# Gate tables written in quarters, one-hot pairs built in two VectorE operations, and late loads issued from ScalarE, in a two-block transformer kernel

## The chip, the cores and the metric

The kernel runs on one core of a Trainium2 chip. The metric is the device time of one execution in microseconds (us), the median of several runs. A profiled execution also leaves a trace of every instruction and every transfer. PE is TensorE's matrix multiply, PEld its weight load, DVE is VectorE, ACT is ScalarE, POOL is GpSimd, SP is SyncE; a trailing q (ACTq, SPq) means an engine's own instruction stream, where it issues transfers.

## The reference

Two blocks run one after the other on 512 tokens of width 1024 in float32. The first mixes tokens and then applies a product-key mixture of 16384 experts, each of which is one row of a table `peer_u` and one row of a table `peer_v`; the second has four mixer layers (pooling, short convolution, latent attention, pooling). The change touches the expert stage alone:

```
q = xb @ w_query                       # 8 heads, two halves of 128 columns
s = q . subkeys                        # 128 scores for each half
sv, si = top_k(s, 16)                  # best 16 of each half
top_s, pos = top_k(all 256 sums, 16)   # best 16 experts of each head
gates = softmax(top_s)                 # 8 heads x 16 = 128 gates for a token
hid = gelu(u_table[experts] . xb) * gates
y   = hid @ v_table[experts]
```

## The kernel before

**Two ways to the same sum.** For the first 384 tokens (ND) the kernel does not gather experts. It multiplies all 16384 rows of the U table with the tokens, applies gelu, multiplies by a dense gate table (zero where an expert isn't chosen) and multiplies with all of the V table. That is 128 U tiles of 128 experts and 128 V tiles. The last 128 tokens are served by gathering: 128 U rows and 128 V rows of 512 KB for all of them, fetched by GpSimd and folded in by one VectorE operation each (line 737 for U, 743 and 745 for V; class `Few`, called with `few.upto`).

**Every weight tile** is loaded by SP (line 139, three buffers `wraw`), rounded by ScalarE into `whi` (141) and completed by VectorE as `wlo` (143); a product is three matmuls (147 to 149), so that a U or V tile is 24 matmuls of 384 columns. `next_w` keeps two tiles ahead of the one in work (`AHEAD`).

**`peer_early`.** After 16 query tiles, `experts_x` scales each of eight chunks of the tokens, splits it into `xh` and `xl` for the 384 tokens, and turns the other 128 tokens with PE (806) into `few.xg`. Then a loop over 96 U tiles (EARLY) does in each pass, in this order: matmuls of one U tile, gelu into `hid` (1002), a store of two tiles to `hid_d` in memory (1004), what the list `pend` holds, at most one gathered row, and then a portion of side work on VectorE, at least SIDE units of it. The side work is a list of generators: top-k of the four token groups, and `all_gates`, which builds the dense gates of a group of 128 tokens in blocks of eight tokens. A block is four VectorE operations (two for `oj` and `oe`, a comparison of positions with indices, 968 and 969; two for `oi`, multiplied by the gates' high and low parts, 972). In the next pass PE multiplies the block's one-hots (16 short matmuls, 979 and 980), ScalarE writes two results into `stg` (982), and after four blocks, ScalarE issues two stores of 1 MB from `stg` to `g_d` (988). `turn` (935) transposes the top-k's result on PE, and ScalarE copies it out; it stands in `pend`, so it runs in the pass after the one that ends a top-k.

**`peer_late`.** It works through eight groups of 16 tiles, first groups 6 and 7, whose U tiles were not done early (32 U tiles, with gelu at 1072 and gates at 1040), and then groups 0 to 5, whose results are read back. The V tiles of a group are two halves of eight tiles. In the second half before a group that was done early (`fetch`), each V tile also loads `hh` (1084, two U results) and every second tile loads `g` (1050, gates of four U tiles). Both are issued on SP, in program order with the weight tiles. Six halves are such fetching halves. Numbers in FEW_RATE spread the remaining gathered rows over the tiles: per tile 1.3 shares beside a U tile, 1.6 beside a plain V tile and 0.3 beside a fetching one.

No scheduler reorders this part: each engine runs in the order in which the code issues (`manual_schedule`).

Of the kernel before, what the change touches and what calls it, by code (L numbers as in the profile page):

```python
# [42 lines left out]
SIDE = 2.6  # L43
AHEAD = 2
EARLY = 96
FEW_EARLY = 64
# [33 lines left out]
def tile_model(ctx: ExitStack, tc: tile.TileContext, xT, cst, vec, pos, w_in, w_tok, w_out, w_q, subk,  # L80
# [674 lines left out]
    def peer_early(bp, hid_d, g_d, ahead, next_w, few):  # L755
        sk = bp.tile([128, 128, GB], F32, name="stg", bufs=2).rearrange("p (h c) n -> p h (c n)", h=32)[:, :16]
# [40 lines left out]
        def experts_x():  # L797

            pt = None
# [42 lines left out]
        iT = bp.tile([128, ND], F16, name="iT")  # L842
        jT = bp.tile([128, ND], F16, name="jT")
        gT = bp.tile([128, ND], F16, name="gT")
        gL = bp.tile([128, ND], F16, name="gL")

        def topk(tt):
# [82 lines left out]
            ts_ = slice(tt * 128, tt * 128 + 128)  # L930

            def turn():
# [3 lines left out]
                scalar.copy(iT[:, ts_], pt[:, 0:128])  # L936
                scalar.copy(jT[:, ts_], pt[:, 128:256])
                scalar.activation(gT[:, ts_], pt[:, 256:384], AF.Copy, scale=GSCALE)
                scalar.activation(gf[tt], pt[:, 256:384], AF.Copy, scale=GSCALE)

            gf[tt] = bp.tile([128, 128], F32, name="gf", bufs=2)
            pend.append(turn)
# [3 lines left out]
        def all_gates(tt):  # L946
            ts_ = slice(tt * 128, tt * 128 + 128)
            vector.tensor_sub(gL[:, ts_], gf.pop(tt), gT[:, ts_])
            yield 0.3
            for nb in range(tt * 128 // GB, (tt + 1) * 128 // GB):  # L950
                yield from gates(nb)

        def gates(nb):


            stg = bp.tile([128, 128, GB], F32, name="stg", bufs=2)
            for h8 in range(GB // HB):
                ns = slice(nb * GB + h8 * HB, nb * GB + (h8 + 1) * HB)
                sh = [128, HB // 2, 128, 2]

                def pairs(t):
                    return t[:, ns].rearrange("p (a o b) -> p a o b", o=1, b=2).to_broadcast(sh)

                places = iotax[:, None, :, :].to_broadcast(sh)
                oj = bp.tile(sh, F16, name="oj", bufs=2)
                oe = bp.tile(sh, F16, name="oe", bufs=1)
                oi = [bp.tile(sh, F16, name="oi%d" % q, bufs=2) for q in range(2)]
# [6 lines left out]
                def dense(oj=oj, oi=oi, h8=h8, q4=0):  # L974
                    ps = ptile()
                    for q in range(4):
                        pq = ps[:, q * 128:(q + 1) * 128]
                        n = q4 * 4 + q
                        tensor.matmul(pq, oj[:, n // 2, :, n % 2], oi[0][:, n // 2, :, n % 2], start=True, stop=False)
                        tensor.matmul(pq, oj[:, n // 2, :, n % 2], oi[1][:, n // 2, :, n % 2], start=False, stop=True)  # L980
# [11 lines left out]
                yield 1.4  # L992

        pend = []
        hid = [None]
# [18 lines left out]
        while side or pend:  # L1014
            now, pend[:] = pend[:], []
            for f in now:
                f()
            some(2.4)
        return xn

    def peer_late(bp, hid_d, g_d, order, next_w, xn, few):
# [23 lines left out]
        queue = []  # L1045

        def get_gates(gr):

            t = bp.tile([128, ND // GB, 4, GB], F32, name="g", bufs=2)
            sync.dma_start(t, g_d[gr])  # L1050
            queue.append(t)

        gates_of = [4 * gr + i for gr in order for i in range(4)]

        def gates(q):

            if q % 4 == 0:
                if q or not queue:
                    queue and queue.pop(0)
                while len(queue) < 2 and gates_of:  # L1060
                    get_gates(gates_of.pop(0))
            return queue[0]

        parts = []
        for n, gr in enumerate(order):
            if gr * 16 >= EARLY:
                parts = []
                for q in range(16):
# [4 lines left out]
                    parts += weighted([a[:, :ND]], gates(q), q % 4)  # L1073
                    slot(0)
                queue.pop(0)
# [599 lines left out]
```

## Time and profile before

| | before |
|---|---|
| median of 3 runs | 3272.76 us (3271.66 to 3275.04) |
| the profiled execution's own time | 3275.82 us |
| its span, first to last instruction | 3274.1 us |
| PE busy | 3148.1 us, 96% of the span |
| DVE / ACT / POOL busy | 2199.2 / 1189.6 / 529.8 us |
| moved by DMA | 525.03 MB, 160 GB/s over the span |

The span is 1.7 us shorter than the execution's own time, which holds what lies around it. A busy PE does not mean that PE runs at its peak: the granted clock has two levels, 1.2 and 2.4 GHz, shown as 0.5 and 1.00 of full speed, and a stretch's clock is the mean of both. The expert stage lies between about 330 and 1721 us of the span; the early loop runs from 480 to 993 us and the late part from there to 1721 us.

### The profile page before, as it was taken

Reading aid. Unit: us, or ns where it says so; the run is one execution under the profiler, and the core shown is the slowest. Engines: PE = TensorE matmul, PEld = TensorE weight load, DVE = VectorE, ACT = ScalarE, POOL = GpSimd, SP = SyncE. Lnnn points to the kernel's source line nnn. Section 1 sums busy time; section 2 is a strip of 40 time slices with the busy share of each in tenths; the row PEclk is TensorE's granted clock in tenths of the full one; section 3 lists DMA queues with packets and bytes.
Section 4 is the critical chain, followed back from the end, with each engine's and each line's share of the span. In section 5 each row is a group of like instructions: output and inputs, shape, how many; then the busy total and the mean of one; then the engine's idle time right before and its main releaser. Section 6 shows DMA issues by size and latency. Waiting matters only on the chain.

```text
span 3274.1 us, 42422 instructions
## 1 busy us (share of the span) xinstructions
PE 3148.1 (96%) x16233; PEld 2720.5 (83%) x16233; DVE 2199.2 (67%) x3983; ACT 1189.6 (36%) x1785; POOL 529.8 (16%) x490
## 2 busy tenths in 40 slices
PE   8999989899998999999999999999999999999998
PEld 7787869888988999998997888888888777778887
DVE  5466779989776888887787665445446655666564
ACT  3334323354553333333334223222224434443222
POOL 2121100121113543332232001000002100010001
PEclk9999989999999999999999999999999999999999
DMA  3211215788888978888882222323332212222331
GB/s 114 71 59 36 88 64 181 238 283 264 268 275 299 372 280 334 324 330 314 320 281 85 96 95 95 94 95 93 96 97 69 71 58 72 72 82 90 97 97 64
DMA packets 194011, 525.03 MB, mean 160 GB/s; under 512 B 16656, under 2 KB 71184, under 8 KB 193680
## 3 DMA queue, kind: packets, MB, share of 16 engines
q1 hardware_dynamic: 99072, 341.86, 31.2%
q0 software_dynamic: 38144, 136.33, 12.0%
q10 hardware_dynamic: 56592, 44.13, 4.1%
q8 instruction: 127, 2.08, 0.3%
q14 instruction: 76, 0.62, 0.1%
HBM read 474.03 MB, written 46.14 MB: 159 GB/s over the span
## 4 chain that ended last, share of the span: by engine, by line
PE 61%; issue 20%; DVE 7%; POOL 6%; DMA 4%; ACT 2%; ACTq 0%; POOLq 0%; DVEq 0%
PE mm L147 18%; PE mm L149 18%; PE mm L148 17%; POOL row L724 5%; DMA row<-in_v_rows_dram,gi 4%; DVE wlo L143 2%; PE mm L1473 1%; PE mm L1440 1%; DVE row L737 1%; PE mm L438 1%; PE mm L1442 1%; PE mm L1459 1%; PE mm L177 0%; POOL acc L193 0%; DVE xg L745 0%
## 5 line engine op out<-in xcount | busy, mean ns | idle before, releaser
L147 PE MATMUL mm<-xh,whi 128*128 128x512 f32 (+2 forms) x2640 | 995.9, 377 | 14.4 <-ACT whi L141 10.3
L141 ACT CAST whi<-wraw 128x1024 fp32r<-128x1024 f32 (+1 forms) x586 | 588.4, 1006 | 1112.0 <-PE mm L148 489.8
L149 PE MATMUL mm<-xh,wlo 128*128 128x512 f32 (+2 forms) x2640 | 976.7, 370 | 15.9 <-DVE wlo L143 15.7
L148 PE MATMUL mm<-xl,whi 128*128 128x512 f32 (+2 forms) x2640 | 971.6, 368 | 1.7 <-DVE xl L227 1.6
L143 DVE TENSOR_TENSOR wlo<-wraw,whi 128x1024 fp32r<-128x1024 f32 (+1 forms) x586 | 687.3, 1174 | 345.6 <-ACT whi L141 344.0
L149 PEld LDWEIGHTS mm<-xh,wlo 128*128 128x128 f32 x2640 | 501.5, 190 | 90.0 <-DVE wlo L143 24.7
L147 PEld LDWEIGHTS mm<-xh,whi 128*128 128x128 f32 x2640 | 502.7, 190 | 83.5 <-ACT whi L141 12.2
L148 PEld LDWEIGHTS mm<-xl,whi 128*128 128x128 f32 x2640 | 502.8, 190 | 66.3 <-DVE xl L227 3.8
L149 PE MATMUL mm<-mh,wlo 128*128 128x384 f32 x1024 | 348.5, 340 | 11.3 <-DVE wlo L143 11.2
L147 PE MATMUL mm<-mh,whi 128*128 128x384 f32 x1024 | 347.0, 339 | 12.5 <-ACT whi L141 12.5
L148 PE MATMUL mm<-ml,whi 128*128 128x384 f32 x1024 | 345.8, 338 | 0.0
L724 POOL DMA_INDIRECT row<-in_u_rows_dram,gi x128 | 160.1, 1251 | 621.9 <-DVE row L737 386.8
L724 POOL DMA_INDIRECT row<-in_v_rows_dram,gi x128 | 173.1, 1352 | 347.7 <-DVE xg L745 317.4
L149 PEld LDWEIGHTS mm<-mh,wlo 128*128 128x128 f32 x1024 | 194.7, 190 | 19.8 <-DVE wlo L143 19.3
L147 PEld LDWEIGHTS mm<-mh,whi 128*128 128x128 f32 x1024 | 194.7, 190 | 16.0 <-ACT whi L141 16.0
L147 PE MATMUL mm<-mxh,whi 128*128 128x512 f32 x512 | 204.4, 401 | 0.0
L148 PE MATMUL mm<-mxl,whi 128*128 128x512 f32 x512 | 202.0, 395 | 0.0
L149 PE MATMUL mm<-mxh,wlo 128*128 128x512 f32 x512 | 201.9, 394 | 0.0
L237 DVE TENSOR_TENSOR H<-H,mm 128x512 f32<-128x512 f32 x144 | 98.8, 686 | 149.4 <-PE mm L149 149.0
L148 PEld LDWEIGHTS mm<-ml,whi 128*128 128x128 f32 x1024 | 194.8, 190 | 0.0
L745 DVE SCALAR_TENSOR_TENSOR xg<-row,actg,xg 128x1024 f32<-128x1024 f32 x127 | 163.5, 1288 | 24.4 <-DMA row<-in_v_rows_dram,gi 22.9
L737 DVE SCALAR_TENSOR_TENSOR row<-row,xg 128x1024 f32<-128x1024 f32 x128 | 154.7, 1218 | 5.6 <-DMA row<-in_u_rows_dram,gi 5.6
(357 smaller groups left out, 3848.4 us busy)
## 6 DMA issues: line engine op xcount, KB each, us to landing
wraw<-in_u_t_dram SPq DMA_DIRECT2D x128, 512.0 KB, 4.6
wraw<-in_v_t_dram SPq DMA_DIRECT2D x128, 512.0 KB, 6.2
wraw<-in_pw_in_dram SPq DMA_DIRECT2D x64, 512.0 KB, 3.5
wraw<-in_cw_in_dram SPq DMA_DIRECT2D x64, 512.0 KB, 3.5
g_d<-stg ACTq DMA_DIRECT2D x24, 1024.0 KB, 8.8
g<-g_d SPq DMA_DIRECT2D x32, 768.0 KB, 5.9
hid_d<-hid ACTq DMA_DIRECT2D x48, 384.0 KB, 5.1
hh<-hid_d SPq DMA_DIRECT2D x48, 384.0 KB, 5.4
```

The lines of the kernel that those rows point to most:

```text
L141: scalar.copy(hi[:, :n], raw[:, :n])
L143: vector.tensor_sub(lo[:, :n], raw[:, :n], hi[:, :n].bitcast(F32))
L147: tensor.matmul(ps, sh, mh, start=start, stop=False)
L148: tensor.matmul(ps, sh, ml, start=False, stop=False)
L149: tensor.matmul(ps, sl, mh, start=False, stop=stop)
L237: vector.tensor_tensor(h[2 * dp + e], h[2 * dp + e], ps, op=OP.add)
L438: tensor.matmul(pl[:, j * 64:(j + 1) * 64].rearrange("p (n b) -> p n b", b=b), kf[:, tiles[j]], pairs_of(q[:, j * 128:(j + 1) * 128], b)[: ...
L724: gpsimd.indirect_dma_start(out=t, out_offset=None, in_=table, in_offset=bass.IndirectOffsetOnAxis(ap=self.gi[:, j:j + 1], axis=0))
L737: vector.scalar_tensor_tensor(t, t, 1.0, self.xg, op0=OP.mult, op1=OP.mult, accum_out=hid[:, j:j + 1])
L745: vector.scalar_tensor_tensor(y, t, act[:, j:j + 1], y, op0=OP.mult, op1=OP.add)
L1440: tensor.matmul(ps[:, :nk], qn[e][:, qs], kn[e][:, :nk], start=True, stop=False)
L1442: tensor.matmul(ps[:, :nk], qr[e][rows, qs], krl[rows, :nk], start=False, stop=True)
```

## The change

1. A block's one-hots are two operations of 2048 elements instead of four of 1024: `oh` holds both comparisons and `og` both products; indices and gates lie in `keys` and `gts`, with the pairs side by side. A half block counts 1.25 units of side work instead of 1.4; SIDE goes from 2.6 to 2.75.
2. The store of a `stg` tile is four pieces of 512 KB, kept in a list `outs`. Each pass issues one piece right after its U tile; when a new `stg` tile is begun, all that are left are issued.
3. `turn` goes to a list `later` and runs one pass later.
4. FEW_EARLY goes from 64 to 48: 48 gathered rows in the early loop, 208 in the late part.
5. The late loads of `g` and `hh`: two of each are issued by SP at the start of the late part, every further one by ScalarE, right after it has used up the buffer's contents.
6. The eight token transposes leave `experts_x`: ScalarE copies the chunks aside, and `turn_x` transposes them after the second U tile.

```diff
-SIDE = 2.6
+SIDE = 2.75
-FEW_EARLY = 64
+FEW_EARLY = 48
...
                 xn.append(split(t[:, :ND], ND))
-                if kt % 4 == 0:
-                    pt = ptile()
-                tensor.transpose(pt[:, kt % 4 * 128:(kt % 4 + 1) * 128], t[:, ND:512], ident)
-                if kt % 4 == 3:
-                    scalar.copy(few.xg[:, (kt - 3) * 128:(kt + 1) * 128], pt)
+                scalar.copy(xt[:, kt], t[:, ND:512])
+
+        def turn_x():
+
+            for q in range(2):
+                pt = ptile()
+                for kt in range(4):
+                    tensor.transpose(pt[:, kt * 128:(kt + 1) * 128], xt[:, q * 4 + kt], ident)
+                scalar.copy(few.xg[:, q * 512:(q + 1) * 512], pt)
...
-            pend.append(turn)
+            later.append(turn)
...
+            while outs:
+                scalar.dma_start(*outs.pop(0))
             stg = bp.tile([128, 128, GB], F32, name="stg", bufs=2)
             for h8 in range(GB // HB):
...
-                vector.tensor_tensor(oj, places, pairs(jT), op=OP.is_equal)
-                vector.tensor_tensor(oe, places, pairs(iT), op=OP.is_equal)
-                yield 1.4
-                for q, g in enumerate((gT, gL)):
-                    vector.tensor_tensor(oi[q], oe, pairs(g), op=OP.mult)
+                oh = bp.tile(sh, F16, name="oh", bufs=2)
+                og = bp.tile(sh, F16, name="og", bufs=2)
+                vector.tensor_tensor(oh, iotax[:, None, None, :, :].to_broadcast(sh), pairs(keys), op=OP.is_equal)
+                yield 1.25
+                vector.tensor_tensor(og, oh[:, 0:1].to_broadcast(sh), pairs(gts), op=OP.mult)
...
-                        for half in range(2):
-                            bs = slice(half * 16, half * 16 + 16)
-                            scalar.dma_start(g_d[bs, :, nb].rearrange("b p i n -> p b (i n)"), src[:, bs])
+                        for z in range(4):
+                            outs.append((g_d[z * 8:z * 8 + 8, :, nb].rearrange("b p i n -> p b (i n)"),
+                                         src[:, z * 8:z * 8 + 8]))
...
-            now, pend[:] = pend[:], []
+            now, pend[:], later[:] = pend[:], later[:], []
             u_tile(e)
+            if e == 1:
+                turn_x()
+            if outs:
+                scalar.dma_start(*outs.pop(0))
...
+        for _ in range(2):
+            get_gates(sync)
+            get_hid(sync)
+
+        def gated(srcs, q):
+
+            r = weighted(srcs, gq[0], q % 4)
+            if (q + len(srcs)) % 4 == 0:
+                gq.pop(0)
+                get_gates(scalar)
+            return r
...
-                    if fetch:
-                        hh = bp.tile([128, 2, ND], F32, name="hh", bufs=2)
-                        sync.dma_start(hh, hid_d[nxt * 8 + q2])
...
                     if fetch:
-                        coming += weighted([hh[:, q] for q in range(2)], gates(q2 * 2), q2 * 2 % 4)
+                        hh = hq.pop(0)
+                        coming += gated([hh[:, q] for q in range(2)], q2 * 2)
+                        get_hid(scalar)
```

How the order moves is shown at three places. On PE at the end of `experts_x`, before (L777 are the scores of a query tile, L806 the token transposes, L147 to L149 the first U tile):

```order
L777 MATMUL mm<-stg,qT 128x128 x4
L806 MATMUL mm<-ident,sq 128x128 x8
L777 MATMUL mm<-stg,qT 128x128 x4
L147 MATMUL mm<-xh,whi 128x384
L148 MATMUL mm<-xl,whi 128x384
L149 MATMUL mm<-xh,wlo 128x384
```

And the same place of the changed kernel (L779 are the scores):

```order
L779 MATMUL mm<-stg,qT 128x128 x8
L147 MATMUL mm<-xh,whi 128x384
L148 MATMUL mm<-xl,whi 128x384
L149 MATMUL mm<-xh,wlo 128x384
L147 MATMUL mm<-xh,whi 128x384
```

The last scores and the first U tile no longer stand behind the eight transposes, which now follow the second U tile.

On ScalarE where a `stg` tile of the first token group is full, before (L982 fills `stg`, L988 stores it, L141 rounds a weight tile, L1002 is gelu):

```order
L982 ACTIVATE stg_5754<-mm_6039 128x4x128 [waits PE_49]
L982 ACTIVATE stg_5754<-mm_6049 128x4x128 [waits PE_49]
L988 DMA g_d_2976<-stg_5754 128x16x128 [waits Activation_49]
L988 DMA g_d_2976<-stg_5754 128x16x128
L141 CAST whi_6075<-wraw_6073 128x1024 [waits DMAHW2_49,DVE_49]
L1002 ACTIVATE hid_6103<-mm_6072 128x384 [waits DMAHW1_49,PE_49]
```

And of the changed kernel, where the second `stg` tile of that group is full and the third is begun (L986 fills `stg`, L962 stores what was left, L1008 is gelu, L1010 the store of `hid`):

```order
L986 ACTIVATE stg_5950<-mm_6161 128x4x128 [waits PE_49]
L962 DMA g_d_2976<-stg_5760 128x8x128 x2
L962 DMA g_d_2976<-stg_5950 128x8x128 [waits DMAHW3_49,Activation_49]
L962 DMA g_d_2976<-stg_5950 128x8x128 [waits DMAHW4_49]
L962 DMA g_d_2976<-stg_5950 128x8x128 [waits DMAHW5_49]
L962 DMA g_d_2976<-stg_5950 128x8x128 [waits DMAHW6_49]
L141 CAST whi_6188<-wraw_6186 128x1024 [waits DVE_49]
L1008 ACTIVATE hid_6128<-mm_6185 128x384 [waits PE_49]
L1010 DMA hid_d_2975<-hid_6128 128x768 [waits DMAHW7_49,Activation_49]
L986 ACTIVATE stg_6177<-mm_6218 128x4x128 [waits DMAHW2_49,DMAHW1_49,PE_49]
```

Six pieces stand here in a row, two of one `stg` tile and four of the next, and the first write into the tile after them waits for transfers of the tile whose buffer it takes.

On SP in the late part where the first fetching half begins, before (L139 loads a weight tile, L1084 `hh`, L1050 `g`):

```order
L139 DMA wraw<-in_v_t_dram 128x1024 x10
L1084 DMA hh<-hid_d 128x768
L139 DMA wraw<-in_v_t_dram 128x1024
L1050 DMA g<-g_d 128x1536
L1084 DMA hh<-hid_d 128x768
L139 DMA wraw<-in_v_t_dram 128x1024
L1084 DMA hh<-hid_d 128x768
L139 DMA wraw<-in_v_t_dram 128x1024
```

And on ScalarE of the changed kernel in the same half (L219 rounds the gated results, L1067 loads `g`, L1072 `hh`):

```order
L219 CAST mh<-sq 128x384 x2
L1072 DMA hh<-hid_d 128x768
L141 CAST whi<-wraw 128x1024
L219 CAST mh<-sq 128x384 x2
L1067 DMA g<-g_d 128x1536
L1072 DMA hh<-hid_d 128x768
L141 CAST whi<-wraw 128x1024
```

SP's stream now holds nothing but weight tiles between the start of the late part and its end; the loads of `g` and `hh` stand behind the ScalarE operations that end the use of the buffer that they fill.

## Rows read from the trace of the kernel before

**Rows 1.** Page, part 1: busy time, share of the span, instructions.
```profile
PE 3148.1 (96%) x16233; PEld 2720.5 (83%) x16233; DVE 2199.2 (67%) x3983; ACT 1189.6 (36%) x1785; POOL 529.8 (16%) x490
```
**Rows 2.** By stretch: length; busy PE, PEld, DVE, ACT, POOL; PE clock, DMA share, GB/s.
```profile
460.00:480.00 20.00, 6.14 (x24) 3.55 (x22) 15.47 (x51) 4.75 (x9) 0.00 (x0) 0.67 0.03 12
...
660.00:763.00 103.00, 95.11 (x695) 91.50 (x696) 87.98 (x152) 62.20 (x77) 20.02 (x18) 0.98 0.92 293
763.00:812.00 49.00, 41.92 (x235) 39.28 (x234) 46.60 (x121) 18.64 (x26) 6.77 (x7) 0.97 0.74 241
812.00:993.00 181.00, 169.71 (x1257) 162.87 (x1255) 131.32 (x193) 105.46 (x126) 23.65 (x21) 0.97 0.87 267
993.00:1032.00 39.00, 30.82 (x158) 29.16 (x157) 23.00 (x35) 11.49 (x20) 14.78 (x10) 0.89 0.88 311
...
993.00:1721.00 728.00, 690.33 (x3834) 672.47 (x3832) 582.28 (x747) 244.84 (x333) 269.13 (x194) 0.98 0.86 318
```
**Rows 3.** The same view: a plain V half, then two fetching halves with their ends.
```profile
1370.00:1403.00 33.00, 33.00 (x193) 33.00 (x192) 29.05 (x29) 8.06 (x9) 18.99 (x14) 1.00 0.98 375
1403.00:1443.00 40.00, 37.03 (x201) 35.88 (x200) 30.07 (x45) 16.12 (x24) 3.63 (x3) 0.96 0.75 275
...
1476.00:1516.00 40.00, 34.82 (x182) 32.42 (x180) 26.96 (x42) 15.03 (x23) 3.18 (x3) 0.96 0.77 275
```
**Rows 4.** ScalarE in order of time: start, duration, idle before and its releaser.
```profile
508.42 0.49 ACT L1002 ACTIVATE hid<-mm 128x384 f32<-128x384 f32 x1 [2.76 <-PE mm L149]
...
512.61 0.49 ACT L1002 ACTIVATE hid<-mm 128x384 f32<-128x384 f32 x1 [2.19 <-PE mm L149]
...
689.51 4.31 ACTq L988 DMA_DIRECT2D g_d<-stg  x2
693.92 1.05 ACT L141 CAST whi<-wraw 128x1024 fp32r<-128x1024 f32 x1 [4.44 <-issue]
...
725.77 0.49 ACT L1002 ACTIVATE hid<-mm 128x384 f32<-128x384 f32 x1 [1.72 <-PE mm L149]
...
730.96 0.49 ACT L1002 ACTIVATE hid<-mm 128x384 f32<-128x384 f32 x1 [1.72 <-PE mm L149]
```
**Rows 5.** One line's transfers: duration ns of issuing, min/median/max, first and last start.
```profile
L988 ACTq DMA_DIRECT2D g_d<-stg x24: 377/860/5013, 689.5 to 988.3; - x24
```
**Rows 6.** Waits of PE in the early loop: us in total, times, longest.
```profile
PE mm L935 <- DVE ij L906: 9.1, 3, 3.4
...
PE mm L935 <- DVE ij L924: 3.7, 3, 1.3
```
**Rows 7.** Groups of instructions, the whole span: busy us, mean ns.
```profile
L737 DVE SCALAR_TENSOR_TENSOR row<-row,xg 128x1024 f32<-128x1024 f32 x128 | 154.7, 1218 | 5.6 <-DMA row<-in_u_rows_dram,gi 5.6
L982 ACT ACTIVATE stg<-mm 128x512 f32<-128x512 f32 x96 | 100.3, 1158 | 26.2 <-PE mm L149 10.8 <-PE mm L980 9.4 <-issue 6.0
...
L968 DVE TENSOR_TENSOR oj<-iotax,jT 128x1024 f16<-128x1024 f16 x48 | 32.7, 682 | 0.6 <-PE mm L980 0.6
...
L901 DVE TENSOR_TENSOR rb<-rb,sf 128x1024 f16<-128x1024 f16 x16 | 19.6, 1225 | 0.5
```
**Rows 8.** The turn to the late part on VectorE, in order of time.
```profile
1004.34 0.56 DVE L1040 TENSOR_TENSOR sq<-acc,g 128x384 f32<-128x384 f32 x1 [7.90 <-DMA g<-g_d]
```
**Rows 9.** Waits of SP's queue from 1000 to 1740 us: total, times, longest.
```profile
SPq L1050 <- DVE sq L1040: 134.4, 23, 9.9
SPq L1084 <- DVE sq L1040: 94.6, 19, 10.7
```
**Rows 10.** A fetching half on ScalarE, its first and last rounding, in order of time.
```profile
1402.14 1.05 ACT L141 CAST whi<-wraw 128x1024 fp32r<-128x1024 f32 x1
...
1433.09 1.05 ACT L141 CAST whi<-wraw 128x1024 fp32r<-128x1024 f32 x1 [1.62 <-DMA wraw<-in_v_t_dram]
```
**Rows 11.** Page, part 6: transfers, KB each, median us to landing.
```profile
wraw<-in_v_t_dram SPq DMA_DIRECT2D x128, 512.0 KB, 6.2
...
hh<-hid_d SPq DMA_DIRECT2D x48, 384.0 KB, 5.4
```

More of the change, by code (lines that the diff above doesn't have):

```diff
@@ L755, in peer_early @@
     def peer_early(bp, hid_d, g_d, ahead, next_w, few):
-        sk = bp.tile([128, 128, GB], F32, name="stg", bufs=2).rearrange("p (h c) n -> p h (c n)", h=32)[:, :16]
+        room = bp.tile([128, 128, GB], F32, name="stg", bufs=2).rearrange("p (h c) n -> p h (c n)", h=32)
+        sk = room[:, :16]
+        xt = room[:, 16:24]
         sync.dma_start(sk, subk)
@@ L840, in peer_early @@
         side.append(list_scores(15, last))
[L842 to L845, printed above, removed]
+        keys = bp.tile([128, ND // HB, 2, HB], F16, name="keys")
+        gts = bp.tile([128, ND // HB, 2, HB], F16, name="gts")
         def topk(tt):
@@ L935, in turn @@
                     tensor.transpose(pt[:, a * 128:(a + 1) * 128], ij[:, a], ident)
[L936 to L941, printed above, removed]
-            pend.append(turn)
+                for a in range(2):
+                    scalar.copy(keys[:, bs, a], pt[:, a * 128:(a + 1) * 128].rearrange("p (n b) -> p n b", b=HB))
+                pg = pt[:, 256:384].rearrange("p (n b) -> p n b", b=HB)
+                scalar.activation(gts[:, bs, 0], pg, AF.Copy, scale=GSCALE)
+                scalar.activation(gf[tt], pg, AF.Copy, scale=GSCALE)
+            gf[tt] = bp.tile([128, 128 // HB, HB], F32, name="gf", bufs=2)
+            later.append(turn)
         gf = {}
         def all_gates(tt):
-            ts_ = slice(tt * 128, tt * 128 + 128)
-            vector.tensor_sub(gL[:, ts_], gf.pop(tt), gT[:, ts_])
+            bs = slice(tt * 128 // HB, (tt + 1) * 128 // HB)
+            vector.tensor_sub(gts[:, bs, 1], gf.pop(tt), gts[:, bs, 0])
             yield 0.3
@@ L978, in dense @@
                         n = q4 * 4 + q
-                        tensor.matmul(pq, oj[:, n // 2, :, n % 2], oi[0][:, n // 2, :, n % 2], start=True, stop=False)
-                        tensor.matmul(pq, oj[:, n // 2, :, n % 2], oi[1][:, n // 2, :, n % 2], start=False, stop=True)
+                        for g in range(2):
+                            tensor.matmul(pq, oh[:, 1, n // 2, :, n % 2], og[:, g, n // 2, :, n % 2], start=g == 0,
+                                          stop=g == 1)
                     o = h8 * HB + q4 * 4
@@ L985, in dense @@
                         src = stg.rearrange("p (b i) n -> p b (i n)", b=32)
-                        for half in range(2):
-                            bs = slice(half * 16, half * 16 + 16)
-                            scalar.dma_start(g_d[bs, :, nb].rearrange("b p i n -> p b (i n)"), src[:, bs])
+                        for z in range(4):
+                            outs.append((g_d[z * 8:z * 8 + 8, :, nb].rearrange("b p i n -> p b (i n)"),
+                                         src[:, z * 8:z * 8 + 8]))
                 for q4 in range(HB // 4):
                     pend.append(lambda q4=q4, f=dense: f(q4=q4))
-                yield 1.4
+                yield 1.25
         pend = []
+        later = []
+        outs = []
         hid = [None]
@@ L1013, in peer_early @@
             some(SIDE)
-        while side or pend:
-            now, pend[:] = pend[:], []
+        while side or pend or later:
+            now, pend[:], later[:] = pend[:], later[:], []
             for f in now:
                 f()
+            if outs:
+                scalar.dma_start(*outs.pop(0))
             some(2.4)
+        for o in outs:
+            scalar.dma_start(*o)
         return xn
@@ L1043, in weighted, with get_gates, get_hid @@
             return [split(m[:, :ND], ND, tagp="m", pool=bp, bufs=MBUFS) for m in ms]
[L1045 to L1051, printed above, removed]
-        gates_of = [4 * gr + i for gr in order for i in range(4)]
[L1055 to L1062, printed above, removed]
+        gq, hq = [], []
+        gates_of = [4 * gr + i for gr in order for i in range(4)]
+        hid_of = [gr * 8 + i for gr in order if gr * 16 < EARLY for i in range(8)]
+        def get_gates(eng):
+            if gates_of:
+                gq.append(bp.tile([128, ND // GB, 4, GB], F32, name="g", bufs=2))
+                eng.dma_start(gq[-1], g_d[gates_of.pop(0)])
+        def get_hid(eng):
+            if hid_of:
+                hq.append(bp.tile([128, 2, ND], F32, name="hh", bufs=2))
+                eng.dma_start(hq[-1], hid_d[hid_of.pop(0)])
+        for _ in range(2):
[7 more added lines that the diff above has]
+            return r
         parts = []
@@ L1072, in peer_late @@
                     scalar.activation(a[:, :ND], ps[:, :ND], AF.Gelu)
-                    parts += weighted([a[:, :ND]], gates(q), q % 4)
+                    parts += gated([a[:, :ND]], q)
                     slot(0)
-                queue.pop(0)
             coming = []
```

17 lines of the change are left out of this document (5 added, 12 removed).

## The prediction

> **What bounds the kernel now.** I read the page first: PE is busy for 96% of the span [rows 1]. So the kernel's time is PE's work plus what PE loses, and the change has to be judged by PE's losses in the expert stage. Next I split that stage into stretches and read the idle part of PE and its granted clock in each [rows 2]. A stretch loses its idle time, and on top of it busy time multiplied by what the clock lacks to 1.00.
>
> To know the floor I need the pace of an undisturbed tile. Two gelus that follow each other at a place where PE never waits are 512.61 - 508.42 = 4.19 us apart; where a block of gates stands beside each tile, 730.96 - 725.77 = 5.19 us [rows 4]. So a U tile costs PE 4.19 us, a block 1.00 us, and a V tile, with as many matmuls, about 4.19 us too. The early loop has 96 tiles and 48 blocks: 450 us of the 513 between 480 and 993. The late part has 160 tiles: 670 us of the 728 [rows 2]. Some 60 us are lost in each; nothing else in the program is touched.
>
> Where they are lost: at 460 to 480 PE is busy for 6.14 of 20 us while the token chunks are made; in the last top-k (763 to 812) it is idle for 7.1 us; where the late part begins (993 to 1032) for 8.2 us at a clock of 0.89 [rows 2]. In the late part the plain V halves lose nothing (33.00 of 33.00 busy), but the fetching halves with their ends lose 3.0 and 5.2 of 40 us at a clock of 0.96 [rows 3].
>
> **The change, part by part.**
>
> *Token transposes later.* PE's first U tile needs each chunk's `xh` and `xl`, of which one comes every 2 us or so; today it stands behind eight transposes that need the last chunk. Afterwards 21 of its 24 matmuls run while chunks are made: 7/8 x 4.19 = 3.7 us, and the last scores with them. The transposes return behind tile 1. I know no row of them at full clock; as matmuls of a third of the columns they cost between a third of 4.19/24 each, 0.5 us in all, and three times that. Scores gained and transposes lost about cancel. **-3 us**, bounds -4 and -2.
>
> *`turn` a pass later.* PE waits 9.1 + 3.7 = 12.8 us before line 935, at three places [rows 6]. One pass later the results have long been there. What is late next is VectorE: in the top-k stretches its busy share is the higher one (46.60 of 49 against PE's 41.92 [rows 2]), so after the first of the three places the wait only moves to `wlo`. The other two are followed by gate tiles, where PE sets the pace. Two thirds are 8.5 us, less what VectorE takes back: **-7 us** with a little clock, bounds -14 and 0.
>
> *48 gathered rows instead of 64.* Counted in the order of VectorE, the last top-k's eight tiles hold four rows instead of six. At 1.22 us each [rows 7], in a stretch that VectorE bounds: **-2 us**, bounds -5 and 0.
>
> *One-hots and quarters.* Four operations of 0.68 us become two of 2048 elements [rows 7]. Nothing in the trace has that size; if they keep the rate they cost at most 2 x 0.68 us, so a block stays at 2.7 us at most, and I count nothing for it. What counts is the order: three half blocks now fit into a pass where there were two, so the 48 blocks stand in about 32 tiles instead of 48. PE's sum is unchanged. Per such tile PE needs 4.19 + 1.5 = 5.7 us. ScalarE needs 1.05 for `whi`, 0.49 for gelu, 3 x 1.16 for `stg` [rows 4, 7], and 0.38 for each transfer that goes in freely [rows 5], 5.6 to 5.8 us: as much as PE. VectorE needs 1.2 + 0.6 + 1.5 x 2.7 = 5.9 us at most. So the new gate tiles are balanced on a knife's edge, where the old ones had ScalarE free for a fifth of the time.
>
> Stores: today a pair of 1 MB takes ScalarE 4.31 us, and `whi` behind it starts 4.44 us late [rows 4]; that is twelve times. One piece a pass would cost ScalarE the 0.38 us of the shortest issue [rows 5]. But the order shows three places where six pieces are issued in a row, 3 MB. If a first 1 MB goes in freely, and each further one takes what the second of a pair takes now, 4.31 - 0.38 = 3.9 us, that is 8 us of ScalarE, three times, and after it the new `stg` tile waits for a transfer. PE has about two tiles, 8 to 10 us, in hand before it misses `whi`. Best case: all that PE loses in both gate stretches (7.9 + 11.3 us idle, less the 8.5 counted above, and 7 of clock) returns, -18. Worst: three bursts in full and the waits behind them, +27. **0 us.**
>
> *Start of the late part.* Today the first load of `g` waits for the last gate store; VectorE waits 7.90 us for it [rows 8], and `wlo` behind it. Afterwards the gates are stored some 15 tiles before the loop ends, and `g` is there. The stretch loses 8.2 + 0.11 x 30.8 = 11.6 us [rows 2]. **-10 us**, bounds -12 and -4.
>
> *`g` and `hh` on ScalarE.* SP waits 134.4 + 94.6 us for VectorE to free their buffers, with the weight tiles queued behind [rows 9]. The circle in a fetching half: the gate product frees `hh`, SP loads it and only then issues a weight tile, which lands after 6.2 us [rows 11], is rounded and completed (1.05 + 1.2), and only then does VectorE come to the gate product of two tiles later. That is about 10 us for two tiles, and seven roundings in a row are indeed (1433.09 - 1402.14)/6 = 5.16 us apart [rows 10], against 4.19. Eight tiles fall 8 us behind, of which PE's lead hides a part. The loss is 3.0 + 1.5 and 5.2 + 1.4 us [rows 3], 5.5 on average; six halves are 33 us. Afterwards SP issues a weight tile as soon as a buffer is free. ScalarE's own loads wait for nothing: the rounding just before them needed the same products. A second circle stays: product, two roundings (1.0 us), load, landing (5.4 us), 8 to 9 us for two tiles, close to the 8.4 that PE needs. **-28 us**, bounds -33 and 0.
>
> The Trainium skill (DMA: Bandwidth & Descriptors, "Issuing engines are not separate DMA queues") says the opposite: transfers of all issuing engines share the same DMA engines, and a second issuer only saves the time of issuing, which is usually small. By it this part would be worth next to nothing; here the time saved is not that of issuing but of a wait at the head of SP's queue.
>
> *16 rows more in the late part.* 16 x 1.22 = 20 us of VectorE at most. Plain V halves have room for them: 29.05 of 33 us busy [rows 3]. Beside the 32 late U tiles (1.2 for `wlo`, 1.1 for product and split, 1.5 rows instead of 1.4) VectorE comes to 4.2 us, PE's own pace. **+4 us**, bounds 0 and +20.
>
> Sum: -3 - 7 - 2 + 0 - 10 - 28 + 4 = -46. The profiled execution took 3275.82 us, which gives 3229.8; it lies 3.1 us above the median of the runs, so for the median I take **3227 us**.
>
> **The rivals.**
>
> *ScalarE bounds the gate tiles.* For it: the balance above, and bursts of 3 MB. Against it: it is idle in the passes around. Price: its worst case, +27: 3254 us. Chance 0.17.
>
> *The late part is bound by transfers.* A plain V half already keeps the DMA engines busy for 0.98 of the time, at 375 GB/s [rows 3]. A fetching tile at PE's pace needs 0.52 + 0.39 + 0.39 MB and a third of a row, 1.5 MB in 4.19 us or 350 GB/s, where now 275 flow; `wraw` would land later and two thirds of the 28 us would stay lost. Against it: that very half shows PE without a gap at 375. Price +19: 3246 us. Chance 0.13. By the rule of the Trainium skill above all 28 would be lost, 3255 us.
>
> *Both together.* +46, no change to speak of: 3273 us. Chance 0.05.
>
> *The one-hots fall to the slow rate (slower).* Line 901, also 1024 halves of 16 bits but with another pattern in its second source, takes 1225 ns where 968 takes 682 [rows 7]. If the wider patterns fall to that rate, an operation takes 2.4 us, a gate tile costs VectorE 1.2 + 0.6 + 7.2 = 9 us against PE's 5.7, and 32 of them lose 106 us, of which the other parts return 46: 3333 us. It decides from about 1.9 us for an operation; at 1.36 it is nothing. Against it: the pairs still lie side by side. Chance 0.04.
>
> **How the numbers follow.** The forecast has 0.61, with a range of its own from 3205 to 3245, by the bounds of its parts taken as independent. A measurement of this kernel can't tell 0.2%, 6.5 us, from no change. Forecast and the first two rivals are faster; of the third I give most to same and some to slower; the fourth is slower: faster 0.89, same 0.05, slower 0.06. The range for 8 in 10 reaches from 3198 to the first rival with some room, 3260; it leaves out the last two rivals and the tails.
>
> **What would show it.** In the changed kernel: the first gelu 5 us earlier against the chunks; no wait of PE before the transposes of `turn`; blocks in about 32 tiles with a pace of 5.7 to 6.2 us, and some 15 plain tiles of 4.19 us behind them; operations of 2048 elements at 1.2 to 1.36 us; at the three bursts, 7 to 9 us of ScalarE's queue; no wait for `g` at the late start; in the fetching halves roundings 4.2 to 4.4 us apart and 340 GB/s or more, with SP waiting for `wlo` alone. I am wrong if PE stands still for more than 4 us at each burst, or if the fetching halves keep a pace near 5 us, because transfers land later or the second circle closes at 9 us or more.

## The result, and the profile after

The changed kernel takes 3228.63 us (median of 4 runs, 3225.60 to 3233.49), the kernel before beside it 3273.65; the ratio is 0.9864 with a 95% interval from 0.9847 to 0.9881, so the changed kernel is 1.4% faster. The forecast was 3227 us. The profiled execution took 3233.49 us with a span of 3231.8, 42.3 less than before. So the sum came out; its terms did not, as will be seen.

Page, part 1, of the changed kernel, which answers to [rows 1]:

```profile
PE 3133.5 (97%) x16233; PEld 2715.0 (84%) x16233; DVE 2195.7 (68%) x3887; ACT 1191.6 (37%) x1793; POOL 550.1 (17%) x490
```

By stretch, with the columns of [rows 2]: the token chunks; the first gate tiles; a top-k; the other gate tiles; the plain tiles; the turn to the late part; all of the late part; and at last a plain V half and a fetching one, as in [rows 3]:

```profile
460.00:480.00 20.00, 14.07 (x39) 7.84 (x39) 15.01 (x46) 7.09 (x18) 0.00 (x0) 0.63 0.00 0
655.00:735.00 80.00, 68.08 (x534) 65.70 (x535) 65.81 (x88) 51.74 (x63) 11.00 (x7) 0.91 0.74 224
735.00:776.00 41.00, 40.17 (x232) 39.96 (x231) 38.68 (x106) 16.59 (x22) 3.75 (x4) 1.00 0.86 282
776.00:908.00 132.00, 113.78 (x908) 109.45 (x908) 103.89 (x102) 83.38 (x101) 16.05 (x10) 0.92 0.79 245
908.00:983.00 75.00, 75.00 (x473) 74.68 (x471) 35.73 (x39) 33.02 (x42) 9.17 (x9) 1.00 0.89 296
987.00:1026.00 39.00, 39.00 (x226) 39.00 (x225) 30.41 (x46) 17.72 (x28) 19.69 (x13) 1.00 0.88 320
987.00:1678.00 691.00, 676.85 (x3850) 667.52 (x3848) 598.39 (x776) 245.21 (x334) 298.82 (x209) 1.00 0.93 341
1272.00:1305.00 33.00, 31.55 (x182) 31.23 (x182) 30.23 (x29) 9.38 (x9) 19.04 (x14) 1.00 0.98 366
1305.00:1342.00 37.00, 36.56 (x211) 36.24 (x210) 31.09 (x49) 16.86 (x25) 4.41 (x4) 1.00 0.94 337
```

The late part is 37 us shorter than in [rows 2], and its start loses nothing now (39.00 of 39). The plain tiles lose nothing either. But the two gate stretches stand idle for 11.9 and 18.2 us, at clocks of 0.91 and 0.92. The one-hots are not the reason; by tile and shape they keep the fast rate, a pair in 2.4 us:

```profile
L975 DVE TENSOR_TENSOR og<-oh,gts 128x2048 f16<-128x2048 f16 x48 | 58.7, 1223 | 1.0
L973 DVE TENSOR_TENSOR oh<-iotax,keys 128x2048 f16<-128x2048 f16 x48 | 58.5, 1218 | 3.9 <-PE mm L983 3.9
```

The reason is a burst. ScalarE in order of time, where six pieces are stored (compare the pair in [rows 4]):

```profile
691.91 2.32 ACTq L962 DMA_DIRECT2D g_d<-stg  x2
...
694.57 7.96 ACTq L962 DMA_DIRECT2D g_d<-stg  x4
702.57 1.04 ACT L141 CAST whi<-wraw 128x1024 fp32r<-128x1024 f32 x1 [8.03 <-DMA g_d<-stg]
```

VectorE at the same place:

```profile
693.50 1.22 DVE L973 TENSOR_TENSOR oh<-iotax,keys 128x2048 f16<-128x2048 f16 x1
703.65 1.23 DVE L143 TENSOR_TENSOR wlo<-wraw,whi 128x1024 fp32r<-128x1024 f32 x1 [8.94 <-ACT whi L141]
704.79 1.22 DVE L737 SCALAR_TENSOR_TENSOR row<-row,xg 128x1024 f32<-128x1024 f32 x1
...
705.94 1.22 DVE L975 TENSOR_TENSOR og<-oh,gts 128x2048 f16<-128x2048 f16 x1
```

And PE:

```profile
700.95 0.34 PE L149 MATMUL mm<-xh,wlo 128*128 128x384 f32 x1
707.22 1.89 PE L983 MATMUL mm<-og,oh 128*128 128x128 f16 x16 [5.93 <-DVE og L975]
...
823.20 1.89 PE L983 MATMUL mm<-og,oh 128*128 128x128 f16 x16 [7.21 <-DVE og L975]
...
894.04 1.89 PE L983 MATMUL mm<-og,oh 128*128 128x128 f16 x16 [6.06 <-DVE og L975]
```

The reader sees the chain: the stores hold `whi` for 8.03 us, `wlo` waits 8.94 us for it, and `og`, which PE needs next, stands behind that `wlo`, and behind a gathered row (line 737), in VectorE's order. PE lives for 9.6 us on the two weight tiles that it had in hand when the burst began (its matmuls run to 701.29 us). What it then waits for is `og`, until 707.22; the next weight tile is complete before that, at 704.88 (703.65 + 1.23). The other two bursts stop PE for 7.2 and 6.1 us.

SP's queue from 1000 to 1740 us; both rows of [rows 9] are gone, and SP waits for `wlo` almost alone, which is the pace of the work:

```profile
SPq L139 <- DVE wlo L143: 658.1, 167, 18.2
SPq L139 <- DVE rs_t L169: 7.4, 1, 7.4
SPq L139 <- DMA wraw<-in_v_t_dram: 6.1, 11, 1.3
```

Roundings of a fetching half on ScalarE, the first and the seventh, as in [rows 10]: (1335.78 - 1309.15)/6 = 4.44 us apart instead of 5.16. The transfers land later than in [rows 11] (page, part 6), without harm in the fetching halves, where PE is busy for 36.56 of 37 us:

```profile
1309.15 1.05 ACT L141 CAST whi<-wraw 128x1024 fp32r<-128x1024 f32 x1
...
1335.78 1.05 ACT L141 CAST whi<-wraw 128x1024 fp32r<-128x1024 f32 x1
```

```profile
wraw<-in_v_t_dram SPq DMA_DIRECT2D x128, 512.0 KB, 6.5
...
hh<-hid_d ACTq DMA_DIRECT2D x46, 384.0 KB, 6.8
```

### The profile page after: what moved, and what is told of

It is laid out like the page before. It is cut to its first block, busy times and chain, and to the rows that moved or that the text cites. A ratio compares the mean times of both kernels' runs of the same rounds, so it can differ in the third digit from the quotient of the medians.

```text
span 3231.8 us, 42341 instructions
## 1 busy us (share of the span) xinstructions
PE 3133.5 (97%) x16233; PEld 2715.0 (84%) x16233; DVE 2195.7 (68%) x3887; ACT 1191.6 (37%) x1793; POOL 550.1 (17%) x490
## 4 chain that ended last, share of the span: by engine, by line
PE 66%; issue 15%; DVE 8%; POOL 5%; DMA 4%; ACT 2%; ACTq 0%; POOLq 0%; DVEq 0%
PE mm L147 20%; PE mm L149 19%; PE mm L148 19%; POOL row L724 4%; DMA row<-in_v_rows_dram,gi 2%; DVE wlo L143 2%; DMA hh<-hid_d 1%; PE mm L1491 1%; PE mm L1458 1%; DVE row L737 1%; DVE xg L745 1%; PE mm L438 1%; PE mm L1460 1%; PE mm L1477 1%; PE mm L177 0%
## 5 line engine op out<-in xcount | busy, mean ns | idle before, releaser
L147 PE MATMUL mm<-xh,whi 128*128 128x512 f32 (+2 forms) x2640 | 993.1, 376 | 10.9 <-ACT xh L219 5.9
L149 PE MATMUL mm<-xh,wlo 128*128 128x512 f32 (+2 forms) x2640 | 974.8, 369 | 17.0 <-DVE wlo L143 16.8
L141 ACT CAST whi<-wraw 128x1024 fp32r<-128x1024 f32 (+1 forms) x586 | 588.0, 1006 | 1031.9 <-PE mm L148 492.2
L149 PEld LDWEIGHTS mm<-xh,wlo 128*128 128x128 f32 x2640 | 500.4, 190 | 90.3 <-DVE wlo L143 24.8
L147 PEld LDWEIGHTS mm<-xh,whi 128*128 128x128 f32 x2640 | 500.8, 190 | 82.5 <-ACT xh L219 9.7
L149 PE MATMUL mm<-mh,wlo 128*128 128x384 f32 x1024 | 344.7, 337 | 9.1 <-DVE wlo L143 9.0
L147 PE MATMUL mm<-mh,whi 128*128 128x384 f32 x1024 | 343.1, 335 | 0.5 <-ACT whi L141 0.5
L724 POOL DMA_INDIRECT row<-in_u_rows_dram,gi x128 | 176.1, 1376 | 625.4 <-DVE row L737 389.7
L149 PEld LDWEIGHTS mm<-mh,wlo 128*128 128x128 f32 x1024 | 192.8, 188 | 14.5 <-DVE wlo L143 14.4
L147 PE MATMUL mm<-mxh,whi 128*128 128x512 f32 x512 | 204.4, 401 | 0.0
L149 PE MATMUL mm<-mxh,wlo 128*128 128x512 f32 x512 | 201.9, 394 | 0.0
L147 PEld LDWEIGHTS mm<-mh,whi 128*128 128x128 f32 x1024 | 192.7, 188 | 0.9 <-ACT whi L141 0.8
L745 DVE SCALAR_TENSOR_TENSOR xg<-row,actg,xg 128x1024 f32<-128x1024 f32 x127 | 163.7, 1289 | 16.7 <-DMA row<-in_v_rows_dram,gi 15.4
```

Source lines behind the costliest of these rows:

```text
L141: scalar.copy(hi[:, :n], raw[:, :n])
L147: tensor.matmul(ps, sh, mh, start=start, stop=False)
L149: tensor.matmul(ps, sl, mh, start=False, stop=stop)
L724: gpsimd.indirect_dma_start(out=t, out_offset=None, in_=table, in_offset=bass.IndirectOffsetOnAxis(ap=self.gi[:, j:j + 1], axis=0))
L745: vector.scalar_tensor_tensor(y, t, act[:, j:j + 1], y, op0=OP.mult, op1=OP.add)
```

## The experiments

All times in one table. "Loop" is the time from the first gelu of the early loop to its 96th, "rest" that from there to the end of the span, both in the profiled execution. The loop of the changed kernel runs from 480.65 to 987.25 us, for instance. The start of the loop itself scatters by 6 us (477.8 to 483.8 us in the kernels with part 6), with the stages ahead of it. Without part 6 (the kernel before, e4, g1) the first gelu comes some 5 us later after the first token chunk, so their "loop" lacks 5 us that the others hold. A profiled execution can lie up to 7 us from the median (f1: 3221.21 beside 3214.42), so differences of a few us between loops, or between rests, show nothing by themselves. Each ratio is to the kernel before as run beside it (3273.65 to 3275.03 us).

| kernel | median | ratio to before (95%) | loop | rest |
|---|---|---|---|---|
| before | 3273.65 | 1 | 505.2 | 2281.4 |
| changed kernel | 3228.63 | 0.9864 (0.9847 to 0.9881) | 506.6 | 2244.6 |
| e1 small flush | 3214.60 | 0.9821 (0.9799 to 0.9843) | 489.4 | 2240.9 |
| e1b two pieces a pass | 3212.36 | 0.9809 (0.9786 to 0.9832) | 492.5 | 2241.4 |
| e3 loads on SP, behind the use | 3492.46 | 1.0659 (1.0635 to 1.0684) | 507.0 | 2499.9 |
| e4 part 5 alone | 3229.11 | 0.9864 (0.9842 to 0.9886) | 503.4 | 2234.7 |
| f4 all but part 5 | 3294.24 | 1.0053 (1.0039 to 1.0066) | 506.3 | 2306.2 |
| e2 `turn` in `pend` | 3225.66 | 0.9859 (0.9844 to 0.9874) | 502.5 | 2239.8 |
| f1 e1, 64 rows early | 3214.42 | 0.9819 (0.9806 to 0.9833) | 509.4 | 2227.5 |
| f5 e1, 72 rows early | 3224.64 | 0.9850 (0.9835 to 0.9865) | 509.7 | 2230.9 |
| g1 e1, part 6 undone | 3215.09 | 0.9816 (0.9798 to 0.9834) | 491.1 | 2237.8 |
| g2 e1, two half blocks | 3221.59 | 0.9838 (0.9818 to 0.9858) | 476.2 | 2263.7 |
| g3 e1 and e2 | 3210.57 | 0.9804 (0.9784 to 0.9825) | 486.8 | 2237.1 |
| g4 g3, 42 rows early | 3210.23 | 0.9800 (0.9782 to 0.9818) | 475.9 | 2250.1 |

**The burst: e1 and e1b.** In both, each piece carries its block's number, and a new `stg` tile flushes only those of the buffer that it takes; e1b also issues two a pass.

```diff
-            while outs:
-                scalar.dma_start(*outs.pop(0))
+            while outs and outs[0][0] < nb - 1:
+                scalar.dma_start(*outs.pop(0)[1:])
```

> The changed kernel, but a new stg tile flushes only the pieces that lie in its own buffer: at most two in a row instead of six. Theory A (the burst of six, 3 MB on ScalarE's queue, makes whi late, wlo behind it, and the og of the next block stands behind that wlo on VectorE, so that PE stops three times for 5.9 to 7.2 us and then runs some us at half clock): 19 us of stops and about 10 us of clock are at stake, and I expect 15 to 25 us less than the changed kernel, about 3209 us. Rival B (the gate tiles are bound by ScalarE or VectorE anyway, and a burst only collects what would be lost in small pieces): less than 6 us.

> The same, and each pass issues up to two pieces, so that none is ever flushed. Theory A: as the run with the small flush, 15 to 25 us less than the changed kernel, a little less if two pieces of 512 KB in a row hold ScalarE as the second store of a pair did before (up to 3.9 us each time). Rival B: less than 6 us.

Measured: 14 and 16 us less than the changed kernel, in or near the range that theory A gave; rival B falls. In the traces e1's loop is 17 us shorter, the rest nearly the same. The gate stretches of e1, with the columns of above, lose 6.4 and 7.2 us instead of 11.9 and 18.2, at a better clock:

```profile
655.00:735.00 80.00, 73.56 (x575) 71.43 (x576) 72.49 (x113) 54.25 (x67) 11.96 (x8) 0.96 0.80 253
776.00:908.00 132.00, 124.77 (x1010) 120.46 (x1010) 107.57 (x105) 90.51 (x106) 17.00 (x11) 0.98 0.86 267
```

**Part 5: e3, e4 and f4.** e4 is the kernel before with the late part of the changed one, f4 the changed kernel with the late part of before (the hunks of part 5 in the diff, forwards and backwards). e3 only changes the issuer:

```diff
-                get_gates(scalar)
+                get_gates(sync)
...
-                        get_hid(scalar)
+                        get_hid(sync)
```

> The changed kernel, but every g and hh of the late part is issued by SP again, at the same place in the program. Theory C (part 5 takes waits from the head of SP's queue, worth 28 us): 24 to 33 us more than the changed kernel, about 3257 us, with SP waiting 100 us or more before g and hh. Rival D (the late part got faster because the gates were stored early and two of each are loaded ahead; who issues is nothing): 0 to 8 us more.

> The kernel before, with part 5 alone (two g and two hh loaded ahead by SP, the others issued by ScalarE). Theory C: 24 to 33 us less than the kernel before, about 3245 us, while the 7.9 us wait for g at the start of the late part stays. Rival D: 0 to 8 us less.

> The changed kernel with the late part of the kernel before, so parts 1 to 4 and 6 without part 5. By the sum of the prediction without its -28: 18 us less than the kernel before, 3255 us. Theory C as it stands after the run of part 5 alone (that part gives 45 us by itself, and the gain of the others is eaten by the three bursts and the 16 late rows): 3265 to 3285 us, no change against the kernel before.

Measured: part 5 alone gives 45.6 us (3274.72 beside e4), as much as the whole change, and without it the others make the kernel 0.5% slower. Both figures lie beyond what theory C said; rival D falls, by e4 and by e3, which loads two ahead as well and is slower. e4 and f4 by stretch, over the six fetching halves and the plain ones behind them, where the kernel before has

```profile
1250.00:1691.00 441.00, 417.98 (x2313) 406.67 (x2312) 352.83 (x437) 146.83 (x193) 131.77 (x99) 0.98 0.86 316
```

e4:

```profile
1241.00:1638.00 397.00, 396.56 (x2288) 396.24 (x2287) 353.24 (x437) 146.45 (x192) 141.99 (x101) 1.00 0.94 350
```

and f4:

```profile
1251.00:1707.00 456.00, 424.11 (x2305) 409.43 (x2305) 362.55 (x445) 146.70 (x193) 141.00 (x107) 0.97 0.85 315
```

In e4 the same work takes 44 us less, PE hardly stands still (396.56 of 397 us busy), and the DMA engines move 350 GB/s. In f4 it takes 15 us more than before. The changed kernel has the same 15 us over e4, though its loads are issued by ScalarE:

```profile
1235.00:1647.00 412.00, 403.74 (x2302) 399.69 (x2301) 362.11 (x444) 147.35 (x193) 147.31 (x107) 1.00 0.94 346
```

So part 5 is worth 44 us in this stretch with the other parts (456 to 412) and without them (441 to 397), and the other parts cost it 15 us either way; f1, below, puts most of that on the 16 rows. The turn to the late part is another matter. In e4 the wait for `g` does not stay as it was: SP issues the first `g`, which waits for the last gate store, one weight tile earlier than before, and the turn loses more than in [rows 2]; in f4, with the gates stored early, nearly all of the loss is gone. e4, then f4:

```profile
993.00:1032.00 39.00, 27.39 (x146) 26.56 (x145) 21.04 (x33) 11.69 (x19) 15.14 (x10) 0.82 0.86 305
```

```profile
987.00:1026.00 39.00, 36.57 (x207) 35.62 (x206) 26.21 (x43) 14.17 (x23) 18.80 (x12) 1.00 0.77 280
```

e3 took 235 us more than expected. It is no undoing of part 5, which I had not seen when I wrote its expectation: before, a load of `hh` stood just ahead of the tile that uses it; in e3 it stands behind the use of the tile two ahead, so that the next weight tile waits for one product more. A fetching half takes 62 to 69 us there instead of 37. The stretch shown above takes 616 us: PE is idle for 137 us of them, and its granted clock is down to 0.88:

```profile
1291.00:1907.00 616.00, 479.42 (x2309) 447.67 (x2308) 362.48 (x444) 147.64 (x193) 141.54 (x108) 0.88 0.64 232
```

SP's waits from 1000 to 1740 us in e3:

```profile
SPq L1067 <- DVE sq L1054: 232.5, 25, 14.5
SPq L1072 <- DVE sq L1054: 178.7, 18, 15.0
```

and in f4, close to [rows 9]:

```profile
SPq L1064 <- DVE sq L1054: 137.4, 23, 10.7
SPq L1098 <- DVE sq L1054: 106.2, 19, 12.7
```

Same transfers, same data, same bytes: what differs is what stands behind the waiting issue.

**`turn`: e2 and g3.** e2 is the changed kernel, g3 is e1, each with:

```diff
-            later.append(turn)
+            pend.append(turn)
```

> The changed kernel with turn in the list pend again, one pass earlier. The prediction gave part 3 7 us (0 to 14). Theory G (VectorE is the late one around the top-k; the later turn only moves PE's wait from the transposes to the first one-hots): within 3 us of the changed kernel, PE waits before turn again and less before the dense gates. By the prediction: 7 us more.

> The changed kernel with the small flush and turn in pend. If the two add up as measured apart (14 us and 3 us): 3211 us. If the 3 us were scatter: 3214 us.

Measured: 3 and 4 us less without part 3, which lies within the scatter (the intervals of the ratios overlap), but not 7 more. PE's waits from 640 to 800 us, of e2:

```profile
PE mm L983 <- DVE og L975: 5.5, 2, 5.0
PE mm L939 <- DVE ij L910: 4.3, 2, 3.4
PE mm L939 <- DVE ij L928: 2.6, 2, 1.3
```

and of the changed kernel:

```profile
PE mm L983 <- DVE og L975: 15.4, 6, 5.9
```

The wait before `turn` (L939) turns into one before the first one-hots (one of the 15.4 is a burst). Theory G fits both times and waits.

**Rows: f1, f5 and g4.** f1 is e1 with FEW_EARLY at 64, f5 and g4 change the rule, one after the other:

```diff
-            few.upto(min(few.done + 1, int((e + 1) * FEW_EARLY / EARLY)))
+            few.upto(min(few.done + 1, int((e + 1) * FEW_EARLY / EARLY)) if e < 80 else few.done + 2)
```

```diff
-            few.upto(min(few.done + 1, int((e + 1) * FEW_EARLY / EARLY)))
+            few.upto(min(few.done + 1, (e + 1) // 3 if e < 80 else 256))
```

> The changed kernel with the small flush (3214.6 us) and, on top, 64 gathered rows early again, as before the change. The groups of the late part took 67 to 70 us each there against 65 to 67 in the run of part 5 alone, which has 64 rows early. Theory E (the 16 rows moved to the late part cost it about 16 x 1.22 us on VectorE, not the 4 us of the prediction): the late part gets 10 to 14 us shorter, the early loop 2 to 5 us longer, about 3206 us. Rival F (the late part is slower there for another reason, such as the earlier prefetch of gates or the order of the transfers): the late part keeps its length and the time rises by 2 to 5 us, 3217 to 3220 us.

> The changed kernel with the small flush, and in the last 16 U tiles of the early loop, which stand without side work and in which VectorE is busy for less than half of the time, two gathered rows a pass instead of one every second pass: 72 rows early. Theory E: the late part loses 24 rows, 15 to 22 us of it go, the early loop keeps its length to 3 us, about 3198 us. Rival F: the late part keeps its length, 3214 us. A third way: the rows' transfers (1 MB a tile on top of 0.5 MB of weights, 375 GB/s at PE's pace) hold up the weight tiles of the early loop, and it gets 5 to 15 us longer.

> As the small flush with turn in pend, but the gathered rows of the early loop come one every third pass up to tile 80 (26 instead of 40) and one every pass behind it (16): 42 rows early. A row in the early loop beside side work has cost 1.3 us (21 us for 16 rows), a row in the late part 0.8 us (13 us for 16): 14 rows fewer beside side work give 18 us, 6 more in the late part cost 5, 8 more beside plain tiles cost 0 to 6: 3200 to 3206 us. Rival: the 1.3 us of a row come from meeting the dense tiles alone and fewer rows than 48 give nothing: 3211 to 3218 us.

Measured: in f1 the rest is 13 us shorter, as theory E has it, but the loop is 20 us longer, not 2 to 5; by the medians the two cancel. f1's profiled execution is one of its slow ones and e1's is its fastest, so up to 8 of the 20 us may be theirs; PE's waits from 655 to 930 us, 30.5 us in f1 and 17.8 in e1, say 13. Of the 13 us in the rest, 10 lie in the six plain V halves that follow fetching ones: 30.1 us each on average in f1, 31.7 in e1 (between the additions at the ends of the halves). What the rows cost there, VectorE's time or transfers, the runs don't tell apart: in the plain half of the changed kernel shown above, at a DMA share of 0.98, ScalarE waits for weight tiles most of the time,

```profile
ACT whi L141 <- DMA wraw<-in_v_t_dram: 20.5, 7, 3.9
```

and PE, behind it, loses 1.5 of 33 us. In f5 the rest gets 10 us shorter and the loop 20 longer: the third way. From 907 to 990 us VectorE waits for the rows' transfers,

```profile
DVE row L737 <- DMA row<-in_u_rows_dram,gi: 29.6, 16, 3.4
```

and there is a wait that I had not named. ScalarE where one group of 16 rows ends:

```profile
931.08 0.22 ACT L740 ACTIVATE actg<-hidg 128x16 f32<-128x16 f32 x1 [10.21 <-DVE row L737]
931.16 0.37 ACTq L1019 DMA_DIRECT2D g_d<-stg  x1
931.20 1.03 ACT L141 CAST whi<-wraw 128x1024 fp32r<-128x1024 f32 x1
```

The gelu of the gathered rows waits for the group's last row, and `whi` stands behind it. PE's waits in this stretch come to 11.5 us. In g4 the loop gives 11 us and the rest takes back 13, more than the 5 I had put on six rows; why is open. The time is that of g3.

**The token transposes: g1.** Part 6 undone in e1; `turn_x` is not called.

```diff
-                scalar.copy(xt[:, kt], t[:, ND:512])
+                tensor.transpose(pt[:, kt % 4 * 128:(kt % 4 + 1) * 128], t[:, ND:512], ident)
```

> The changed kernel with the small flush, and the eight token transposes back in experts_x, as before the change (part 6 undone). By the prediction 3 us more than with the small flush alone (bounds 2 and 4); the trace of the changed kernel showed the third gelu 5 us earlier than before, so perhaps 5 us: 3217 to 3220 us. Rival: tiles 1 and 2 of the changed kernel take 5 us each instead of 4.2 and the whole is worth nothing: 3214 us.

Measured: no difference by the medians. In the trace it can be told, from the first chunk on VectorE to the third gelu: 490.68 - 465.10 = 25.6 us in the changed kernel and 28.9 in g1, here in two views:

```profile
463.73 0.73 DVE L804 SCALAR_TENSOR_TENSOR sq<-H,vc,rb 128x512 f32<-128x512 f32 x1
```

```profile
492.65 0.49 ACT L1013 ACTIVATE hid<-mm 128x384 f32<-128x384 f32 x1 [2.24 <-PE mm L149]
```

**Density: g2.** e1 with `yield 1.4` instead of `yield 1.25`, so two half blocks a pass.

> The changed kernel with the small flush, and two half blocks a pass as before the change instead of three (each counted 1.4 units instead of 1.25). Theory H (with the bursts gone, the denser tiles lose only what the trace shows, about 9 us over 32 tiles, and finishing the gates early is worth the wait for g at the late start, about 9 us): 3210 to 3220 us. Rival (density itself is what hurts, ScalarE and VectorE have no slack in a pass of three half blocks): 3200 to 3206 us.

Measured: neither. Density does cost: from 760 to 959 us the gate tiles go at 5.19 us and PE is idle for only 2.9 us, and the loop is 13 us shorter than in e1. But the rest is 23 us longer. SP's own queue where the late part begins:

```profile
944.18 0.33 SPq L139 DMA_DIRECT2D wraw<-in_u_t_dram  x1
971.45 0.33 SPq L1067 DMA_DIRECT2D g<-g_d  x1
...
973.60 10.63 SPq L139 DMA_DIRECT2D wraw<-in_u_t_dram  x4
```

The first `g` waits 26.7 us for the last store of the gates, and SP issues no weight tile for 29 us; PE stands still for 15.4. It is once more the wait at the head of SP's queue. Two half blocks a pass with the first weight tiles ahead of the first `g` might take both gains; it wasn't tried.

The best are g3 and g4, 3210 us, 2.0% faster than before and 0.6% faster than the changed kernel.

## Why the prediction was right, by its own steps

The time was right by luck: errors of the terms cancelled. Part 5 gave 17 us more than forecast; against that, the bursts cost some 15 us that the sum had at nothing, and `turn` gave none of its 7.

*Token transposes*, -3: right, 25.6 us from the first chunk to the third gelu in the changed kernel, 495.86 - 467.02 = 28.8 in the kernel before, and within 0.3 us of these in every trace with or without the part. The medians of g1 and e1 do not show it (0.5 us).

*`turn`*, -7: wrong; nothing, or 3 us lost, which is within the scatter. The failing step is that two of the three places "are followed by gate tiles, where PE sets the pace". There, too, VectorE is late when the gate tiles begin.

*48 rows early*, -2, and *16 rows more late*, +4: both mis-sized. f1 against e1 gives 13 to 20 us for the loop and 13 for the rest; by the medians the sum is nothing. I had counted the rows in the last top-k alone; they also hit the gate tiles, where VectorE has no room, as the prediction's own 5.9 us for PE's 5.7 says. The late 13 lie between 4 and 16 x 1.22 = 20. The step that failed there is "Plain V halves have room for them": those halves are where most of the 13 us are lost.

*One-hots and quarters*, 0: the rate was right, the bursts were not. ScalarE's 8 us came as forecast (7.96), but the step that failed is that PE has about two tiles, 8 to 10 us, in hand "before it misses `whi`". The lead held, for 9.6 us; what PE missed was `og`, queued behind `wlo`. The stops of 5.9, 7.2 and 6.1 us are those by which I had said I would be wrong; so the first rival took place in its part on the bursts, at 14 to 17 us (e1) where its worst case was 27.

*Start of the late part*, -10: right as a place. There 8.2 us and some clock were lost [rows 2], and the wait for `g` [rows 8] is gone; the changed kernel loses nothing. f4 bears the size out: 2.4 us lost where the kernel before loses 11.6.

*`g` and `hh` on ScalarE*, -28: the mechanism was right, the size was not: 45.6 us alone (e4), 65.6 on top of the other parts (f4 against the changed kernel). I had two readings in hand, roundings 5.16 us apart, which puts eight tiles 8 us behind, and the idle time and clock of two windows, 5.5 us a half. I took the second and assumed that PE's lead hides the difference. It hid next to nothing: six halves with the plain ones behind them lost 44 us, 7.3 each. Of these, idle time and clock hold 23.0 + 0.02 x 418 = 31 us; the other 13 lay in busy time (417.98 against 396.56), since a busy PE is not PE at its pace. By the rule of the Trainium skill (DMA: Bandwidth & Descriptors, "Issuing engines are not separate DMA queues") a second issuer saves the time of issuing alone. e4 speaks against it in this place: it gained 45.6 us, and what was saved is a wait at the head of a queue.

*The second rival* (transfers) fell for the fetching halves: `wraw` lands at 6.5 us instead of 6.2, the late part flows at 341 GB/s, e4's halves at 350, with hardly a stop of PE. For the plain halves, which the prediction took as free, it stays open: there the changed kernel's weight tiles come late, as shown under f1.

Together, from the experiments: -3 (transposes), +3 (`turn`), -20 and +13 (rows), +15 (bursts), -10 (start), -45 (part 5) is -47, beside 45 measured. The agreement proves little. These are differences between pairs of kernels, some from traces and some from medians, and they don't add: without part 5 the terms come to -2, and f4 measures 20 us more than before. Part 5 gives 45.6 us alone and 65.6 on top of the others; its 44 us in the fetching halves are the same both times, and of the rest most lies ahead of them, where part 5 alone makes the turn to the late part worse.

## What to carry to other kernels

A load that waits for a consumer to free its buffer belongs where its engine has waited for that consumer anyway (here behind ScalarE's rounding of the product), not ahead of loads that others wait for. The same loads at the same place in the program took 264 us more on SP (e3 against the changed kernel), and 198 us more than in SP's old order (e3 against f4). When a stall is sized, multiply the pace of the tiles by their number: the idle time of a window holds only part of it. A lead in weight tiles protects an engine only if nothing else that it needs stands behind the late tile in a neighbour's order; and a flush should write out what the buffer needs, not all that is there.

## What the hardware showed that I had not expected

Issuing stores in a row held the issuing engine far longer than one issue does: a single 512 KB piece took ScalarE 0.41 us in the median (the 26 of line 1019), four in a row behind two others 7.96 us. What holds it is not shown; it was not SP's issuing, since SP issued nothing from 691.5 to 704.9 us. A small operation that waits can do the same: the 0.22 us gelu of a group of 16 gathered rows kept ScalarE's other work waiting for 10.21 us in f5, `whi` among it. And PE's busy time itself shrank by 5% (417.98 to 396.56 us for the same tiles) once its weights came in time, though the clock had risen by 0.02 only; the profile's busy time can hold part of a stall.
